# Attention scores with the lo parts of the queries on half the array's rows, two matmuls side by side, and the attention stage in a fixed order

## The chip, the cores and the metric

One core of a Trainium2 chip runs the whole kernel: one launch, float32 in and out. The core has five engines that run beside each other, each taking its own list of instructions in order: TensorE (PE, matmuls and transposes; PEld is its weight load), VectorE (DVE), ScalarE (ACT), GpSimd (POOL) and SyncE (SP), which issues transfers. Matmuls write to PSUM, eight banks of 128 x 512 float32; DVE and ACT read from there. The metric is the device time of one execution in microseconds, the median of several runs.

## What is computed

An encoder block over 2048 positions of width 1024: an input projection, differential attention with four heads beside Fourier mixing, an output projection, and a gated MLP. What concerns us here is the attention, cut to its core:

```python
def block(args):                       # one block of 128 queries
    qi, i = args                       # q, k: (B, S, 4 heads, 2 components, 64)
    dist = jnp.abs(pos_q[:, None] - pos_k[None, :])
    s = jnp.einsum('bqhcd,bkhcd->bhcqk', qi, k) * scale
    s = s - slopes[None, :, None, None, None] * dist[None, None, None]
    p = jax.nn.softmax(s, axis=-1)
    a = p[:, :, 0] - lam * p[:, :, 1]
    return jnp.einsum('bhqk,bkhv->bqhv', a, v)
```

Every head has two components c of queries and keys, each 64 wide. Each gives its own 128 x 2048 scores and softmax; the second, scaled by lam, is taken from the first, and the difference weighs the values.

## The kernel before, in words

To keep float32 accuracy with matmuls that round their operands, every operand is split in a hi part (rounded) and a lo part (what is left); products of hi with hi, hi with lo and lo with hi are summed. `split` (L77) makes the two: ACT copies hi out (L81), DVE subtracts to get lo (L82), so a lo always waits for its hi. `mm3` (L119) issues the three matmuls.

`in_proj` writes queries and keys to scratch in memory (`qd`, `kd`), transposed, each head and component as 64 rows of hi and 64 rows of lo. `load_k` brings a head's keys to SBUF so that partitions 0 to 63 hold hi and 64 to 127 lo. `load_q` puts the same 64 query rows on both halves of the partitions. One matmul of 128 rows with the hi part of the queries so gives hi x hi + hi x lo; one with the lo part gives lo x hi, and lo x lo beside it.

The attention stage runs over 64 units (4 heads times 16 blocks of 128 queries), in steps t, four to a unit; n = t // 4 is the unit whose scores are made. For a unit n:

- `scores` (L543): for each component c and each half of the keys (1024 wide), four matmuls (L567) into a PSUM tile s of two banks; there are two such tiles. DVE then adds slope times distance and keeps the running minimum mn (L572; `red0` for the first half, `red1` for the second, whose start value is red0's minimum). After the second half ACT takes the exponential over all 2048 columns with mn as bias and sums it (L576).
- `combine` (L579): DVE makes 1/sum (rr, L583) and the coefficient cf (L585); POOL and ACT scale the second component (L441, L443, L444) and POOL adds the two (L589).
- `transposes` (L591), two units later: four groups g of four 128 x 128 transposes into a PSUM tile pt (two tiles), each followed by a `split`: hi on ACT, lo on DVE. They give the transposed weights `at`.
- `values` (L602): `mm3` of `at` with the values of the head, two units (a pair) at a time, six matmuls 256 wide in each step.
- `finish` (L611): squares and scales a pair's output.

Tile positions, buffers and waits come from the framework. It also puts the instructions in each engine's order, by its own reckoning of when things are ready; `issue_after` (L130) ties one instruction behind another on the same engine where the author wants it. Before the change the attention stage has no such tie in its inner work, and the order is the framework's. While the first two units run, Fourier mixing still goes on (`fourier`, which advances the stage by `next(attention)`).

Of the kernel before, what the change touches and what calls it, by code (L numbers as in the profile page):

```python
# [11 lines left out]
F32 = mybir.dt.float32  # L12
# [3 lines left out]
AF = mybir.ActivationFunctionType  # L16
ALU = mybir.AluOpType
# [3 lines left out]
P = 128  # L21
D = 1024
S = 2048
NB = S // P
KB = D // P
H = 4
DH = 64
# [3 lines left out]
HALF = 512  # L31
# [4 lines left out]
SLOPES = [2.0 ** (-8.0 * (h + 1) / H) for h in range(H)]  # L36
# [4 lines left out]
class Block:  # L41
# [76 lines left out]

    def mm3(self, ps, terms, first=True, last=True, again=False):  # L119


        mm = functools.partial(self.nc.tensor.matmul, ps, skip_group_check=again)
        n = len(terms)
        for i, (ah, al, bh, bl) in enumerate(terms):
            mm(ah, bh, start=first and i == 0, stop=False)  # L125
            mm(ah, bl, start=False, stop=False)  # L126
            r = mm(al, bh, start=False, stop=last and i == n - 1)  # L127
        return r
# [9 lines left out]
    def in_proj(self, es_u, es_f):  # L138
# [3 lines left out]
        with ExitStack() as es, ExitStack() as es01:  # L142
# [47 lines left out]
            with ExitStack() as esn:  # L190
# [21 lines left out]
                r = {}  # L212
# [37 lines left out]
            for blk, b, gs in ((1, 0, range(4)), (1, 1, range(4)), (0, 0, (0, 1)), (0, 1, (0, 1)),  # L250
# [7 lines left out]
                for g in gs:  # L258
                    row = p.tile([P, HALF], F32, tag="row", name=f"row{blk}{b}{g}")
                    nc.sync.dma_start(row, self.rsd[g * HALF:(g + 1) * HALF].partition_broadcast(P))  # L260
                    for hh in range(2):
# [8 lines left out]
                            row, ALU.mult, ALU.mult)  # L270
                        self.split(z, st[:, 0, :], st[:, 1, :])
                        for c in range(2):
                            (nc.scalar if blk or gs[-1] < 3 else nc.sync).dma_start(
                                dst[h, c, :, :, g * HALF:(g + 1) * HALF].rearrange("l d t -> d l t").bitcast(F32),
                                st[c * DH:(c + 1) * DH].bitcast(F32))
# [179 lines left out]
    def load_k(self, h):  # L455
        t = self.slot(self.K_SLOT[h], [2, S], f"k{h}")
        for c in range(2):
            self.nc.gpsimd.dma_start(t[:, c], self.kd[h, c].rearrange("l d t -> (l d) t"))
        return t
# [71 lines left out]
    def attention(self, pss):  # L531

        nc, a = self.nc, self.a
        with ExitStack() as es:
# [7 lines left out]

            def scores(n, c, half):  # L543
                h, i = units[n]
                if c == 0 and half == 0:
                    if i % 4 == 2 and n + 2 < NU:
# [13 lines left out]
                if half == 0:  # L560
                    zs[n, c] = zp.tile([P, S], F32, tag=f"z{c}", name=f"z{n}_{c}")
                zt, qt, kt = zs[n, c], qs[h, i // 4], ks[h]
                ps = pss.tile([P, 1024], F32, tag="s", name=f"s{n}_{c}{half}")
                for l in range(2):
                    for j in range(2):
                        k0 = half * 1024 + j * HALF
                        nc.tensor.matmul(ps[:, j * HALF:(j + 1) * HALF], qt[:, 2 * c + l, i % 4 * P:i % 4 * P + P],  # L567
                                         kt[:, c, k0:k0 + HALF], start=l == 0, stop=l == 1)
                d0 = (NB - 1 - i) * P + half * 1024
                m0 = c * 2 + half  # L570

                nc.vector.tensor_tensor_reduce(  # L572
                    zt[:, half * 1024:(half + 1) * 1024], ps, dist[:, d0:d0 + 1024], SLOPES[h],
                    3.0e38 if half == 0 else mn[:, m0 - 1:m0], ALU.add, ALU.min, mn[:, m0:m0 + 1])
                if half == 1:
                    nc.scalar.activation(zt, zt, AF.Exp, bias=mn[:, 2 * c + 1:2 * c + 2], scale=-1.0,  # L576
                                         accum_out=ss[:, c:c + 1])

            def combine(n, half):  # L579
                z, z1, ss, rr = zs[n, 0], zs[n, 1], sums[n][1], recips[n // 2][:, n % 2, :]  # L580
                x = slice(half * 1024, (half + 1) * 1024)
                if half == 0:
                    nc.vector.reciprocal(rr, ss)  # L583
                    cfs[n] = sp.tile([P, 1], F32, tag="cf", name=f"cf{n}")
                    nc.vector.tensor_scalar(cfs[n], ss[:, 0:1], neglam[:, 0:1], rr[:, 1:2], ALU.mult, ALU.mult)  # L585
                    self.scale_half(0, z1[:, x], cfs[n])
                else:
                    self.scale_half(1, z1[:, x], cfs.pop(n))
                nc.gpsimd.tensor_tensor(z[:, x], z[:, x], z1[:, x], ALU.add)  # L589

            def transposes(n, g):  # L591
# [4 lines left out]
                for j in range(4):  # L596
                    kb = g * 4 + j
                    nc.tensor.transpose(pt[:, j * P:(j + 1) * P], zs[n, 0][:, kb * P:(kb + 1) * P], self.ident)  # L598
                us = slice(n % 2 * P, n % 2 * P + P)
                self.split(pt.rearrange("p (j t) -> p j t", j=4), at[:, :, 0, us], at[:, :, 1, us])  # L600

            def values(pr, kbs):  # L602
                h = units[2 * pr][0]
                if kbs[0] == 0:
# [3 lines left out]
                                           ats[pr, kb // 4][:, kb % 4, 1, :]) for kb in kbs],  # L608
                         first=kbs[0] == 0, last=kbs[-1] == NB - 1)

# [44 lines left out]

            LAG, outs, cfs = 2, {}, {}
            for t in range(4 * (NU + LAG + 4)):
                if t < 4 * LAG:
                    yield
                elif t == 4 * LAG:  # L660
# [489 lines left out]
```

## Time and profile before

| what | value |
|---|---|
| median of 3 runs | 2571.65 us (2568.43 to 2571.72) |
| the profiled execution's own time | 2574.7 us |
| its span, first to last instruction | 2572.9 us |
| PE busy | 2516.6 us, 98% |
| PEld busy | 2114.6 us, 82% |
| DVE busy | 1752.6 us, 68% |
| ACT busy | 1301.9 us, 51% |
| POOL busy | 716.9 us, 28% |
| first and last start of a score matmul | 410.3 and 954.8 us |
| first and last start of a transpose of attention | 427.4 and 972.4 us |
| mean granted clock of TensorE | 0.992 |

Lines of the profile's groups name the line of the kernel, the engine, the operation, the tile written and the tiles read, the shape and the count; then the busy time of the group, the mean duration of one in ns, and the idle time ahead of them with what ended it. Lines of a timeline give start and length in us, the same names, and in brackets the idle time just before, with what ended it. Matmuls overlap in the pipeline, so the sum of their lengths is more than the time they take; the step from one start to the next is the better measure. Rows of stretches give the busy time of PE, PEld, DVE, ACT and POOL, then the granted clock, the share of the transfer engines, and GB/s.

### The profile page before, as it was taken

How to read it: one execution, taken by the hardware profiler on the slowest of the kernel's cores; microseconds unless marked ns; L12 is line 12 of the kernel's file. 1: busy time of each engine (PE TensorE's matmuls, PEld its weight loads, DVE VectorE, ACT ScalarE, POOL GpSimd, SP SyncE). 2: the span in 40 equal slices, each digit the busy share in tenths (PEclk: the TensorE clock that was granted, in tenths of full speed). 3: DMA queues.
4: the chain of work that ended last, by engine and by line, in shares of the span. 5: the costliest groups of instructions: out<-in, count | busy, mean ns of one | idle time of the engine just before them, and what ended most of it. 6: DMA issues, size and time to landing. Idle time of an engine off the chain costs nothing.

```text
span 2572.9 us, 34950 instructions
## 1 busy us (share of the span) xinstructions
PE 2516.6 (98%) x13021; PEld 2114.6 (82%) x13021; DVE 1752.6 (68%) x2691; ACT 1301.9 (51%) x2036; POOL 716.9 (28%) x797
## 2 busy tenths in 40 slices
PE   9999999999999999978999999999999999999998
PEld 9998877888888888866888888877888888888886
DVE  4533358988889996786877777657777777434443
ACT  6321246888888883233544454444454445333332
POOL 1300015888988883271010010000000000000000
PEclk9999999999999999988999999999999999999999
DMA  8335558343332205554222221454212222546463
GB/s 264 98 125 139 152 143 237 66 74 73 74 75 50 48 26 173 181 174 140 107 74 79 88 79 70 160 181 155 91 74 76 88 83 85 185 137 219 146 204 113
DMA packets 146154, 309.12 MB, mean 120 GB/s; under 512 B 12080, under 2 KB 69440, under 8 KB 138816
## 3 DMA queue, kind: packets, MB, share of 16 engines
q1 hardware_dynamic: 90816, 226.60, 26.2%
q0 software_dynamic: 18256, 34.57, 6.7%
q10 hardware_dynamic: 36912, 45.72, 5.8%
q8 instruction: 102, 1.67, 0.3%
q14 instruction: 68, 0.56, 0.1%
HBM read 225.05 MB, written 81.80 MB: 119 GB/s over the span
## 4 chain that ended last, share of the span: by engine, by line
PE 87%; DVE 5%; DMA 4%; issue 1%; POOL 1%; ACT 1%; SPq 0%; POOLq 0%; ACTq 0%; DVEq 0%
PE s L567 9%; PE pd L127 5%; PE pd L125 5%; PE pd L126 5%; PE pt L598 4%; PE o L125 3%; PE o L127 3%; PE o L126 3%; PE pz L125 2%; PE pz L127 2%; PE pz L126 2%; DMA hb<-htd 2%; PE pv L127 1%; PE pv L126 1%; PE pv L125 1%
## 5 line engine op out<-in xcount | busy, mean ns | idle before, releaser
L589 POOL TENSOR_TENSOR z<-z,z 128x1024 f32<-128x1024 f32 x128 | 307.1, 2414 | 0.1
L82 DVE TENSOR_TENSOR d<-wd,d 128x512 fp32r<-128x512 f32 x240 | 157.0, 689 | 211.7 <-ACT d L81 211.4
L567 PE MATMUL s<-k,q 128*128 128x512 f32 x1024 | 281.5, 396 | 3.0 <-DVE mn L572 2.0
L576 ACT ACTIVATE z<-z,mn 128x2048 f32<-128x2048 f32 x128 | 257.5, 2012 | 33.7 <-DVE mn L572 32.7
L81 ACT ACTIVATE d<-wd 128x512 fp32r<-128x512 f32 x240 | 141.8, 626 | 236.9 <-PE pd L127 186.2
L125 PE MATMUL pd<-d,d 128*128 128x512 f32 x640 | 251.8, 393 | 1.9 <-ACT d L81 1.4
L127 PE MATMUL pd<-d,d 128*128 128x512 f32 x640 | 251.2, 393 | 0.5 <-DVE d L82 0.5
L126 PE MATMUL pd<-d,d 128*128 128x512 f32 x640 | 251.5, 393 | 0.0
L567 PEld LDWEIGHTS s<-k,q 128*128 128x128 f32 x1024 | 174.5, 188 | 29.4 <-DVE mn L572 5.0
L572 DVE CUSTOM_DVE_ANT_0 z<-s,dist,mn 128x1024 f32<-128x1024 f32 x128 | 163.8, 1280 | 38.6 <-PE s L567 37.8
L82 DVE TENSOR_TENSOR at<-pt,at 128x512 fp32r<-128x512 f32 x256 | 169.9, 686 | 8.5 <-ACT at L81 8.4
L81 ACT ACTIVATE at<-pt 128x512 fp32r<-128x512 f32 x256 | 147.5, 592 | 48.2 <-PE pt L598 44.8
L125 PE MATMUL o<-at,v 128*128 128x256 f32 x512 | 162.0, 316 | 0.0
L598 PE MATMUL pt<-ident,z 128*128 128x128 f32 x1024 | 156.7, 276 | 5.1 <-DVE at L82 5.1
L572 DVE CUSTOM_DVE_ANT_0 z<-s,dist 128x1024 f32<-128x1024 f32 x128 | 155.8, 1217 | 5.4 <-PE s L567 4.4
L598 PEld LDWEIGHTS pt<-ident,z 128*128 128x128 f32 x1024 | 125.7, 144 | 36.3 <-issue 10.5
L98 POOL TENSOR_SCALAR y_rs<-y_rs 128x1 f32<-128x1 f32 x16 | 6.9, 429 | 524.9 <-ACT sq L95 524.9
L126 PE MATMUL o<-at,v 128*128 128x256 f32 x512 | 146.3, 286 | 0.0
L125 PEld LDWEIGHTS pd<-d,d 128*128 128x128 f32 x640 | 120.1, 188 | 30.6 <-ACT d L81 1.8
L127 PEld LDWEIGHTS pd<-d,d 128*128 128x128 f32 x640 | 120.1, 188 | 29.0 <-DVE d L82 1.4
L127 PE MATMUL o<-at,v 128*128 128x256 f32 x512 | 143.7, 281 | 0.0
L126 PEld LDWEIGHTS pd<-d,d 128*128 128x128 f32 x640 | 120.1, 188 | 27.7 <-DVE d L82 0.3
(1058 smaller groups left out, 6895.0 us busy)
## 6 DMA issues: line engine op xcount, KB each, us to landing
wu<-in_w_up SPq DMA_DIRECT2D x44, 1024.0 KB, 4.8
wd<-in_w_down SPq DMA_DIRECT2D x88, 512.0 KB, 3.6
wd<-gd SPq DMA_DIRECT2D x88, 256.0 KB, 3.9
q<-qd POOLq DMA_DIRECT2D x32, 512.0 KB, 7.0
gd<-t SPq DMA_DIRECT2D x22, 512.5 KB, 2.6
gd<-t SPq DMA_DIRECT2D x22, 511.5 KB, 3.1
wst<-in_w_in SPq DMA_DIRECT2D x72, 128.0 KB, 3.6
xt<-in_xt SPq DMA_DIRECT2D x16, 512.0 KB, 4.6
```

Source lines behind the costliest of these rows:

```text
L81: r = nc.scalar.activation(hi, src, AF.Copy)
L82: return r, (lo_engine or nc.vector).tensor_tensor(lo, src, hi.bitcast(F32), ALU.subtract)
L98: nc.gpsimd.tensor_scalar(t[:, 1:2], t[:, 0:1], 1.0 / D, EPS, ALU.mult, ALU.add)
L125: mm(ah, bh, start=first and i == 0, stop=False)
L126: mm(ah, bl, start=False, stop=False)
L127: r = mm(al, bh, start=False, stop=last and i == n - 1)
L567: nc.tensor.matmul(ps[:, j * HALF:(j + 1) * HALF], qt[:, 2 * c + l, i % 4 * P:i % 4 * P + P], kt[:, c, k0:k0 + HALF], start=l == 0, stop=l ...
L572: nc.vector.tensor_tensor_reduce(zt[:, half * 1024:(half + 1) * 1024], ps, dist[:, d0:d0 + 1024], SLOPES[h], 3.0e38 if half == 0 else mn[: ...
L576: nc.scalar.activation(zt, zt, AF.Exp, bias=mn[:, 2 * c + 1:2 * c + 2], scale=-1.0, accum_out=ss[:, c:c + 1])
L589: nc.gpsimd.tensor_tensor(z[:, x], z[:, x], z1[:, x], ALU.add)
L598: nc.tensor.transpose(pt[:, j * P:(j + 1) * P], zs[n, 0][:, kb * P:(kb + 1) * P], self.ident)
```

## The change

Three things change, all for the attention stage.

The scratch of the keys is split in two halves of the sequence, and in the second half hi and lo change places. After loading, partitions 0 to 63 hold hi for the first 1024 keys and lo for the others; partitions 64 to 127 the reverse. The hi x (hi + lo) matmuls use all 128 rows as before. The lo part of the queries now meets only the hi part of the keys, on 64 rows: the upper rows for the first half of the keys, the lower rows for the second. The two halves' lo matmuls follow each other in turn, into different PSUM tiles; lo x lo is no longer computed. `load_k` issues four transfers for a head in place of two.

`scores` makes both halves of a component in one step (every second step), takes both PSUM tiles at once, and then has both reductions. The exponential becomes a function of its own, `exps`, called behind the transposes of the step. Both parts of `combine` are called in the first step of the next unit.

The new `behind` ties the matmuls, transposes and value matmuls on PE, the reductions, reciprocals and lo parts on DVE, and the exponentials and hi parts on ACT in the order in which the code is written.

```diff
-        self.kd = dt("kd", [H, 2, 2, DH, S])
+        self.kd = dt("kd", [H, 2, 2, 2, DH, S // 2])
...
-                        self.split(z, st[:, 0, :], st[:, 1, :])
+                        swap = blk and g // 2
+                        self.split(z, st[:, swap, :], st[:, 1 - swap, :])
...
         for c in range(2):
-            self.nc.gpsimd.dma_start(t[:, c], self.kd[h, c].rearrange("l d t -> (l d) t"))
+            for half in range(2):
+                self.nc.gpsimd.dma_start(t[:, c, half * 1024:(half + 1) * 1024],
+                                         self.kd[h, c, half].rearrange("l d t -> (l d) t"))
...
+            def behind(r, key):
+                if key in last:
+                    self.issue_after(r, last[key])
+                last[key] = r
+                return r
...
-                for l in range(2):
-                    for j in range(2):
-                        k0 = half * 1024 + j * HALF
-                        nc.tensor.matmul(ps[:, j * HALF:(j + 1) * HALF], qt[:, 2 * c + l, i % 4 * P:i % 4 * P + P],
-                                         kt[:, c, k0:k0 + HALF], start=l == 0, stop=l == 1)
...
+                for half in range(2):
+                    for j in range(2):
+                        behind(nc.tensor.matmul(out(half, j), qt[:, 2 * c, u], kt[:, c, cols(half, j)],
+                                                start=True, stop=False), "PE")
+                for j in range(2):
+                    for half in range(2):
+                        r = slice(half * DH, (half + 1) * DH)
+                        behind(nc.tensor.matmul(out(half, j), qt[r, 2 * c + 1, u], kt[r, c, cols(half, j)],
+                                                start=False, stop=True), "PE")
...
-                if half == 1:
-                    nc.scalar.activation(zt, zt, AF.Exp, bias=mn[:, 2 * c + 1:2 * c + 2], scale=-1.0,
-                                         accum_out=ss[:, c:c + 1])
...
+            def exps(n, c):
+                mn, ss = sums[n]
+                behind(nc.scalar.activation(zs[n, c], zs[n, c], AF.Exp, bias=mn[:, 2 * c + 1:2 * c + 2], scale=-1.0,
+                                            accum_out=ss[:, c:c + 1]), "ACT")
...
-                n, c, half = t // 4, t // 2 % 2, t % 2
-                if n < NU:
-                    scores(n, c, half)
+                n = t // 4
+                if n < NU and t % 2 == 0:
+                    scores(n, t // 2 % 2)
...
-                if n < NU and t % 4 == 3:
-                    combine(n, 0)
                 if 0 <= n - LAG < NU:
                     transposes(n - LAG, t % 4)
+                if n < NU and t % 2 == 0:
+                    exps(n, t // 2 % 2)
                 if 0 <= n - 1 < NU and t % 4 == 0:
+                    combine(n - 1, 0)
                     combine(n - 1, 1)
```

How the instructions then stand is shown at unit 32, in the middle of the stage. Names carry the unit and what it is: z32_0 the first component of unit 32, pt30_1 group 1 of the transposes of unit 30, s32_10 the scores of component 1, half 0.

ACT before, from the copy of group 0 to that of the next unit's group 0:

```order
L81 ACTIVATE at30_0_7423<-pt30_0_7424 128x4x128
L443 ACTIVATE z31_1_7353<-z31_1_7353,cf31_7387 128x512
L81 ACTIVATE at30_1_7447<-pt30_1_7448 128x4x128
L576 ACTIVATE z32_0_7407,ss32_7405<-z32_0_7407,mn32_7404 128x2048
L81 ACTIVATE at30_2_7468<-pt30_2_7469 128x4x128
L81 ACTIVATE at30_3_7494<-pt30_3_7495 128x4x128
L576 ACTIVATE z32_1_7461,ss32_7405<-z32_1_7461,mn32_7404 128x2048
L81 ACTIVATE at30_0_7423<-pt31_0_7517 128x4x128
```

And ACT in the change, over the same work:

```order
L82 ACTIVATE at30_0_7430<-pt30_0_7431 128x4x128
L599 ACTIVATE z32_0_7408,ss32_7406<-z32_0_7408,mn32_7405 128x2048
L447 ACTIVATE z31_1_7359<-z31_1_7359,cf31_7440 128x512
L82 ACTIVATE at30_1_7453<-pt30_1_7454 128x4x128
L82 ACTIVATE at30_2_7480<-pt30_2_7481 128x4x128
L599 ACTIVATE z32_1_7467,ss32_7406<-z32_1_7467,mn32_7405 128x2048
L82 ACTIVATE at30_3_7495<-pt30_3_7496 128x4x128
L82 ACTIVATE at30_0_7430<-pt31_0_7524 128x4x128
```

The scaling of the unit before and the copy of group 1 have moved from ahead of the first exponential to behind it, and the copy of group 3 from ahead of the second to behind it.

DVE in the change, from the lo part of group 0 to the first reduction of the next unit (ISA with z is a reduction, ISA with mn alone the read-out of its minimum):

```order
L83 TENSOR_TENSOR at30_0_7430<-pt30_0_7431,at30_0_7430 128x4x128
L606 RECIPROCAL rr30_7207<-ss31_7310 128x2
L608 TENSOR_SCALAR cf31_7440<-ss31_7310,neglam_70,rr30_7207 128x1
L83 TENSOR_TENSOR at30_1_7453<-pt30_1_7454,at30_1_7453 128x4x128
L593 ISA z32_1_7467,mn32_7405<-s32_10_7468,dist_4062 128x1024
L593 ISA mn32_7405 128x1
L593 ISA z32_1_7467,mn32_7405<-s32_11_7469,dist_4062,mn32_7405 128x1024
L593 ISA mn32_7405 128x1
L83 TENSOR_TENSOR at30_2_7480<-pt30_2_7481,at30_2_7480 128x4x128
L83 TENSOR_TENSOR at30_3_7495<-pt30_3_7496,at30_3_7495 128x4x128
L593 ISA z33_0_7511,mn33_7509<-s33_00_7512,dist_4062 128x1024
```

On DVE the lo part of group 1 stands ahead of the second component's reductions and that of group 3 ahead of the next unit's, as before; what has moved is that the first component's two reductions now follow each other directly, with the lo part of group 0, the reciprocal and the coefficient behind both.

PE in the change, a step with scores:

```order
L582 MATMUL s32_00_7409<-k2_6189,q2_0_7202 128x512 x2
L582 MATMUL s32_01_7410<-k2_6189,q2_0_7202 128x512 x2
L587 MATMUL s32_00_7409<-k2_6189,q2_0_7202 128x512
L587 MATMUL s32_01_7410<-k2_6189,q2_0_7202 128x512
L587 MATMUL s32_00_7409<-k2_6189,q2_0_7202 128x512
L587 MATMUL s32_01_7410<-k2_6189,q2_0_7202 128x512
L621 MATMUL pt30_0_7431<-ident_60,z30_0_7208 128x128 x4
L126 MATMUL o14_7385<-at28_1_7253,v1_5784 128x256
```

Before, four score matmuls stood in each step, all of 128 rows; now eight stand in every second one, the last four (L587) of 64 rows each and in turn for the two halves.

More of the change, by code (lines that the diff above doesn't have):

```diff
@@ L117, in transpose_split, with mm3 @@
         return last
-    def mm3(self, ps, terms, first=True, last=True, again=False):
+    def mm3(self, ps, terms, first=True, last=True, again=False, order=lambda r: r):
         mm = functools.partial(self.nc.tensor.matmul, ps, skip_group_check=again)
@@ L124, in mm3 @@
         for i, (ah, al, bh, bl) in enumerate(terms):
-            mm(ah, bh, start=first and i == 0, stop=False)
-            mm(ah, bl, start=False, stop=False)
-            r = mm(al, bh, start=False, stop=last and i == n - 1)
+            order(mm(ah, bh, start=first and i == 0, stop=False))
+            order(mm(ah, bl, start=False, stop=False))
+            r = order(mm(al, bh, start=False, stop=last and i == n - 1))
         return r
@@ L270, in in_proj @@
                             row, ALU.mult, ALU.mult)
-                        self.split(z, st[:, 0, :], st[:, 1, :])
+                        swap = blk and g // 2
+                        self.split(z, st[:, swap, :], st[:, 1 - swap, :])
                         for c in range(2):
+                            d = (dst[h, c, g // 2, :, :, g % 2 * HALF:(g % 2 + 1) * HALF] if blk
+                                 else dst[h, c, :, :, g * HALF:(g + 1) * HALF])
                             (nc.scalar if blk or gs[-1] < 3 else nc.sync).dma_start(
-                                dst[h, c, :, :, g * HALF:(g + 1) * HALF].rearrange("l d t -> d l t").bitcast(F32),
+                                d.rearrange("l d t -> d l t").bitcast(F32),
                                 st[c * DH:(c + 1) * DH].bitcast(F32))
@@ L541, in attention, with scores @@
             zs, sums, recips, ats, pos = {}, {}, {}, {}, {}
-            def scores(n, c, half):
+            def behind(r, key):
[3 more added lines that the diff above has]
+                return r
+            def scores(n, c):
                 h, i = units[n]
-                if c == 0 and half == 0:
+                if c == 0:
                     if i % 4 == 2 and n + 2 < NU:
@@ L569, in scores @@
[L569 to L574, printed above, removed]
-                if half == 1:
-                    nc.scalar.activation(zt, zt, AF.Exp, bias=mn[:, 2 * c + 1:2 * c + 2], scale=-1.0,
-                                         accum_out=ss[:, c:c + 1])
+                mn = sums[n][0]
@@ new lines, in scores @@
+                zt = zs[n, c] = zp.tile([P, S], F32, tag=f"z{c}", name=f"z{n}_{c}")
+                qt, kt = qs[h, i // 4], ks[h]
+                u = slice(i % 4 * P, i % 4 * P + P)
+                ps = [pss.tile([P, 1024], F32, tag="s", name=f"s{n}_{c}{half}") for half in range(2)]
+                cols = lambda half, j: slice(half * 1024 + j * HALF, half * 1024 + (j + 1) * HALF)
+                out = lambda half, j: ps[half][:, j * HALF:(j + 1) * HALF]
+                for half in range(2):
+                    for j in range(2):
+                        behind(nc.tensor.matmul(out(half, j), qt[:, 2 * c, u], kt[:, c, cols(half, j)],
+                                                start=True, stop=False), "PE")
@@ new lines, in scores @@
+                for j in range(2):
[3 more added lines that the diff above has]
+                                                start=False, stop=True), "PE")
+                d0 = (NB - 1 - i) * P
+                for half in range(2):
+                    m0 = c * 2 + half
+                    behind(nc.vector.tensor_tensor_reduce(
+                        zt[:, half * 1024:(half + 1) * 1024], ps[half], dist[:, d0 + half * 1024:d0 + (half + 1) * 1024],
+                        SLOPES[h], 3.0e38 if half == 0 else mn[:, m0 - 1:m0], ALU.add, ALU.min, mn[:, m0:m0 + 1]), "DVE")
@@ L582, in combine @@
                 if half == 0:
-                    nc.vector.reciprocal(rr, ss)
+                    behind(nc.vector.reciprocal(rr, ss), "DVE")
                     cfs[n] = sp.tile([P, 1], F32, tag="cf", name=f"cf{n}")
@@ L597, in transposes @@
                     kb = g * 4 + j
-                    nc.tensor.transpose(pt[:, j * P:(j + 1) * P], zs[n, 0][:, kb * P:(kb + 1) * P], self.ident)
+                    behind(nc.tensor.transpose(pt[:, j * P:(j + 1) * P], zs[n, 0][:, kb * P:(kb + 1) * P], self.ident), "PE")
                 us = slice(n % 2 * P, n % 2 * P + P)
-                self.split(pt.rearrange("p (j t) -> p j t", j=4), at[:, :, 0, us], at[:, :, 1, us])
+                hi, lo = self.split(pt.rearrange("p (j t) -> p j t", j=4), at[:, :, 0, us], at[:, :, 1, us])
+                behind(hi, "ACT")
+                behind(lo, "DVE")
             def values(pr, kbs):
@@ L608, in values @@
                                            ats[pr, kb // 4][:, kb % 4, 1, :]) for kb in kbs],
-                         first=kbs[0] == 0, last=kbs[-1] == NB - 1)
+                         first=kbs[0] == 0, last=kbs[-1] == NB - 1, order=lambda r: behind(r, "PE"))
             def finish(pr, stage):
@@ L654, in attention @@
             loading = {}
-            LAG, outs, cfs = 2, {}, {}
+            LAG, outs, cfs, last = 2, {}, {}, {}
             for t in range(4 * (NU + LAG + 4)):
```

4 lines of the change are left out of this document (removed).

## The prediction

> **What bounds the kernel now.** I read the page first: its span and its busy shares. Then the busy times of the stretch in which attention runs evenly, then the chain of waits in that stretch, and last the timelines of the engines, row by row, over one unit (128 queries of one head).
>
> ```profile
> span 2572.9 us, 34950 instructions
> core 0: us, PE busy (x) PEld busy (x) DVE busy (x) ACT busy (x) POOL busy (x), PEclk, DMA share, GB/s
> 500.00:920.00 420.00, 419.74 (x2848) 373.96 (x2847) 376.24 (x716) 356.49 (x496) 370.06 (x323) 1.00 0.31 61
> by line: PE s L567 43.0%; PE pt L598 21.1%; PE o L125 11.1%; PE o L127 10.9%; PE o L126 10.8%; PE o L624 2.0%; issue 0.7%; DVE z L572 0.4%; DVE at L82 0.2%; DVE mn L572 0.0%; DVE wo_x L82 0.0%
> ```
>
> TensorE is busy all through these 420 us, and the chain is its own instructions, one behind the other: scores, transposes, values. But the others are close: DVE has 376.24 us of work in 420. So what TensorE saves can only be had if the other three still keep up, and an order in which they wait for each other would be seen at once.
>
> The first DVE row of unit 2 and that of unit 63 give the pace:
>
> ```profile
> 428.89 1.21 DVE L572 CUSTOM_DVE_ANT_0 z<-s,dist 128x1024 f32<-128x1024 f32 x1
> ...
> 949.30 1.22 DVE L572 CUSTOM_DVE_ANT_0 z<-s,dist 128x1024 f32<-128x1024 f32 x1
> ```
>
> 520.41 us for 61 units: **8.53 us a unit**. Now one unit on DVE (start, length), and the same time on ACT, with one DVE row more at the end:
>
> ```profile
> 751.16 1.22 DVE L572 CUSTOM_DVE_ANT_0 z<-s,dist 128x1024 f32<-128x1024 f32 x1
> ...
> 752.69 0.69 DVE L82 TENSOR_TENSOR at<-pt,at 128x512 fp32r<-128x512 f32 x1
> 753.30 1.28 DVE L572 CUSTOM_DVE_ANT_0 z<-s,dist,mn 128x1024 f32<-128x1024 f32 x1
> 754.50 0.08 DVE L572 DVE_READ_ACCUMULATOR2_ANT mn<- 128x1 f32 x1
> 754.50 0.69 DVE L82 TENSOR_TENSOR at<-pt,at 128x512 fp32r<-128x512 f32 x1
> 755.38 1.23 DVE L572 CUSTOM_DVE_ANT_0 z<-s,dist 128x1024 f32<-128x1024 f32 x1 [0.18 <-PE s L567]
> 756.52 0.09 DVE L572 DVE_READ_ACCUMULATOR2_ANT mn<- 128x1 f32 x1
> 757.45 1.28 DVE L572 CUSTOM_DVE_ANT_0 z<-s,dist,mn 128x1024 f32<-128x1024 f32 x1 [0.84 <-PE s L567]
> ...
> 758.66 1.28 DVE L82 TENSOR_TENSOR at<-pt,at 128x512 fp32r<-128x512 f32 x2
> 759.86 1.22 DVE L572 CUSTOM_DVE_ANT_0 z<-s,dist 128x1024 f32<-128x1024 f32 x1
> ...
> 761.39 0.69 DVE L82 TENSOR_TENSOR at<-pt,at 128x512 fp32r<-128x512 f32 x1 [0.23 <-ACT at L81]
> ```
>
> ```profile
> 753.73 0.60 ACT L81 ACTIVATE at<-pt 128x512 fp32r<-128x512 f32 x1
> 754.68 2.01 ACT L576 ACTIVATE z<-z,mn 128x2048 f32<-128x2048 f32 x1 [0.35 <-DVE mn L572]
> ...
> 756.69 0.58 ACT L81 ACTIVATE at<-pt 128x512 fp32r<-128x512 f32 x1
> 757.88 0.60 ACT L81 ACTIVATE at<-pt 128x512 fp32r<-128x512 f32 x1 [0.62 <-PE pt L598]
> 758.78 2.01 ACT L576 ACTIVATE z<-z,mn 128x2048 f32<-128x2048 f32 x1 [0.29 <-DVE mn L572]
> ...
> 760.78 0.58 ACT L81 ACTIVATE at<-pt 128x512 fp32r<-128x512 f32 x1
> 762.11 0.60 ACT L81 ACTIVATE at<-pt 128x512 fp32r<-128x512 f32 x1 [0.75 <-PE pt L598]
> 762.60 0.71 ACT L443 ACTIVATE z<-z,cf 128x512 f32<-128x512 f32 x1
> 763.22 0.37 ACT L618 ACTIVATE osq<-o 128x256 f32<-128x256 f32 x1
> ```
>
> I call the two DVE reductions of one pass (one of the two score components c) red0 and red1, ACT's copy of transposed weights hi and DVE's remainder lo, numbered by group. See that the exponential starts as soon as red1 of its pass is read out, and that before it in ACT's queue stand copies that wait for TensorE alone. In this order hi0, hi1 come ahead of the first exponential, hi2, hi3 ahead of the second.
>
> And one step of TensorE:
>
> ```profile
> 754.24 1.10 PE L567 MATMUL s<-k,q 128*128 128x512 f32 x4
> 755.18 0.60 PE L598 MATMUL pt<-ident,z 128*128 128x128 f32 x4
> 755.53 0.37 PE L125 MATMUL o<-at,v 128*128 128x256 f32 x1
> ...
> 756.32 1.09 PE L567 MATMUL s<-k,q 128*128 128x512 f32 x4
> ```
>
> Four score matmuls take 0.94 us (0.235 each), four transposes 0.35, six value matmuls 0.79. The transposes of 755.18 are over by 755.78, yet their copy starts at 756.69, just behind the exponential: ACT takes its instructions strictly as they stand, and a long one ahead holds those behind it.
>
> **The change part by part.** *Matmuls.* Of eight score matmuls of a pass, four (lo part of the queries) now use 64 rows each, two by two. Side by side they save two times 0.235 us a pass, 0.94 us a unit, and leave TensorE 8.53 - 0.94 = 7.59 us of work; one after the other they save nothing. The trace has no such pair, so both ends stay.
>
> *Order.* This is the part that decides. In the change hi1 stands behind the first exponential and hi3 behind the second, while lo1 stands ahead of the second pass's reductions on DVE and lo3 ahead of the next unit's. Before, both stood ahead of those exponentials, and one ring went round once a unit (red1, exponential, hi2, hi3, lo3, next red0, next red1): 1.35 + 2.01 + 0.49 + 0.61 + 0.61 + 2.14 = 7.21 us with the steps below, 762.60 - 762.11 from copy to next and 753.30 - 751.16 from red0 to red1. That is under 8.53, so TensorE set the pace. Now there is a **ring through ACT and DVE, twice a unit**: red0, red1, exponential, hi, lo, and only then the next red0. Its terms, start to start:
>
> - red0 to red1: red0 is read out at 756.52 + 0.09, 1.23 after its start; red1 needs that value, and the nearest row of an instruction that needs a small result of its own engine starts 0.03 us after it (rr, cf below). I take 1.25. Ends: 1.14 if it could start with the read-out, 1.33 with the 0.10 us seen between 754.58 and the exponential.
> - red1 to exponential: 754.68 - 753.30 = 1.38, 758.78 - 757.45 = 1.33. I take 1.35.
> - exponential to the next on ACT: 756.69 - 754.68 = 2.01.
> - in the first pass only, the scaling of the unit before (L443) stands between: 763.22 - 762.60 = 0.62.
> - hi to lo: 761.39 - 760.78 = 0.61.
> - lo to the next reduction: 753.30 - 752.69 = 0.61, and half of 759.86 - 758.66, 0.60.
>
> First pass 1.25 + 1.35 + 2.01 + 0.62 + 0.61 + 0.61 = 6.45; second, without the scaling, 5.83 with 0.61. Sum **12.28 us a unit**, whatever TensorE does in it, since 7.59 or 8.53 both fit. Bounds by the two uncertain terms: 12.28 - 2 x 0.13 = 12.02 and 12.28 + 2 x 0.11 = 12.50.
>
> Does TensorE or POOL lengthen the ring? With red0 at 0, red1 ends at 2.53 and frees the second score buffer; the second pass's scores are done near 3.5 (4.0 one after the other) and needed at 6.45. The next unit's wait for the second pass's red1, over at 6.45 + 2.53 = 8.98, are done near 10.0 and needed at 12.28. POOL has 370.06 / 420 x 8.53 = 7.52 us a unit, starting from cf near 3.5: done near 11, needed by transposes that ACT copies only in the next unit. So none of them stands in the ring, and the whole saving on TensorE lies beside it.
>
> *Keys.* Loading a head's keys takes four transfers in place of two:
>
> ```profile
> L458 POOL DMA_DIRECT2D k<-kd x2 | 1.2, 597 | 0.0
> ```
>
> Two more issues of 0.6 us a head, on a POOL queue that now has some 4 us free a unit: nothing; 1.2 us a head if that were not so. The stores of the keys move as much as before, to other places.
>
> *Ends of the stage.* Before, the last coefficient is ready here:
>
> ```profile
> 958.73 0.17 DVE L583 RECIPROCAL rr<-ss 128x2 f32<-128x2 f32 x1 [0.90 <-ACT z L576]
> 958.93 0.27 DVE L585 TENSOR_SCALAR cf<-ss,neglam,rr 128x1 f32<-128x1 f32 x1
> ```
>
> That is 9.6 us after 949.30. In the change it stands behind the lo of the next step, at 12.28 + 0.6 + 0.2 = 13.1: 3.5 us later, with TensorE's last transposes behind it as before. In two units DVE has an output-weight split between the two reductions of a pass:
>
> ```profile
> 927.96 2.02 DVE L82 TENSOR_TENSOR wo<-wost,wo 128x512 fp32r<-128x512 f32 x1
> ```
>
> Between 0.7 and 2.0 us each in the ring: 2 us.
>
> **Sum.** 61 x (12.28 - 8.53) = 228.8; + 3.5 + 2 = 234 us. Against the profiled execution's own 2574.7 us: 2809. The median of the runs shown, 2571.65, lies 3 us under that execution, so 2806 us, **9% slower**. Bounds of the ring: 61 x 12.02 and 61 x 12.50 put it between 2790 and 2819; 5 us either way for the ends of the stage.
>
> **The rivals.**
>
> *The clock falls.* TensorE now waits in pieces. The longest: group 3 of the transposes needs the buffer that lo1 frees at 5.84 + 0.69 = 6.53 us, while the values ahead are done near 3.5 + 0.35 + 0.79 = 4.65, a gap of 1.9 us (1.4 if the pairs run one after the other). What gaps did in this trace:
>
> ```profile
> 1098.51 1.06 PE L754 MATMUL ht<-ident,hn 128*128 128x128 f32 x8 [1.83 <-ACT ms L81]
> 1770.41 0.50 PE L125 MATMUL pu_0a<-b,a_0p 128*128 128x512 f32 x1 [2.46 <-ACT xg L897]
> 1772.04 0.63 PE L125 MATMUL pu_0a<-b,a_0p 128*128 128x512 f32 x1
> 1771.00:1775.00 4.00, 4.00 (x12) 3.12 (x11) 1.89 (x2) 0.16 (x1) 0.10 (x1) 0.59 0.88 351
> 1100.00:1104.00 4.00, 4.00 (x19) 3.23 (x18) 3.79 (x6) 0.89 (x2) 4.00 (x4) 1.00 0.71 238
> 1800.00:2000.00 200.00, 200.00 (x863) 161.71 (x862) 153.66 (x199) 98.17 (x144) 16.47 (x40) 1.00 0.22 82
> ```
>
> After 1.83 us idle the granted clock stayed at 1.00; after 2.46 it fell to 0.59 over the next 4 us. A gap of 1.9 lies between. At half clock throughout, TensorE would need 2 x 7.59 = 15.2 us a unit, and the stage 61 x (15.2 - 8.53) = 407 us more: 2982. That can't hold, since TensorE without gaps gets its clock back (the 1800 row); with a fall in every second unit the scores are late by some 0.5 us a unit, 2836. I take that as this rival's time. The Trainium skill, TensorE: Matmul & The Clock Gate, Part 1, puts the drop at an idle window of about 3.4 us and asks for no gaps over some 3; by that there is no fall and the forecast stands, but the row of 2.46 us shows one sooner.
>
> *The saving is had.* If the ring did not close, because the copies came ahead of the exponential in time, the stage would go at the pace of the largest load: DVE, 376.24 / 420 x 8.53 = 7.64 us a unit, TensorE's 7.59 just under it. 61 x 0.89 = 54 us off: 2517. It decides from the point where a pass of the ring is under 3.8 us; the five terms make 5.8. For it speaks only that DVE and ACT are both under 90% busy now. The Trainium skill, same page, Part 3, says that matmuls on different row groups run at the same time; that is what TensorE's 7.59 would rest on, and no run here shows it yet. By it alone the kernel gains these 54 us; by the rows it gains nothing, since the ring doesn't pass through TensorE.
>
> *The pairs run one after the other.* TensorE then keeps 8.53 us, still under 12.28. The time is that of the forecast: the clock alone cannot tell, the starts of the paired matmuls can.
>
> **How the numbers follow.** Forecast (pairs side by side or not) 86%; the clock rival 8%; the saving had 3%, nothing changed 1%, and 2% for a longer ring that I haven't seen. The range takes in the ring's bounds and the clock rival: 2784 to 2840. About 0.2% is what a measurement of this kernel can tell from no change: faster 3%, same 1%, slower 96%.
>
> **What would show it.** Right: first reductions of successive units 12.0 to 12.5 us apart. On the ring's clock DVE has done lo0 and cf near 3.5 us and lo2 near 9.6, and starts lo1 at 5.84 and lo3 at 11.67: it idles 2.3 + 2.1 us a unit ahead of lo, waiting for ACT, some 270 us in all. ACT has done hi2 near 6.2 and hi0 of the next unit near 12.2, and the exponentials start at 9.05 and 14.88: about 5 us a unit, 300 us in all, waiting for DVE's mn. Further: TensorE near 62% busy in the stage; the gap ahead of transposes under 2 us and the clock at 1.00. The lo matmuls of a pair starting at nearly one time would show them side by side. Wrong: a unit under 9 us, or hi1 copied ahead of the exponential.

## The result, and the profile after

| | before | after |
|---|---|---|
| median of the runs side by side | 2570.48 us (2568.43 to 2571.72) | 2823.82 us (2820.76 to 2826.40) |
| span of the profiled execution | 2572.9 us | 2821.9 us |
| unit 2 to unit 63 of the stage | 520.41 us, 8.53 a unit | 765.71 us, 12.55 a unit |

The change makes the kernel slower by 9.8%: the ratio of its time to that before is 1.0981, 95% interval 1.0967 to 1.0995. The prediction of 2806 us was 18 us too low; the side and the mechanism were right.

From the page of the changed kernel, the span and the costliest groups of the stage (busy time, mean ns, then idle time ahead of them and whom it waited for):

```profile
span 2821.9 us, 35051 instructions
L599 ACT ACTIVATE z<-z,mn 128x2048 f32<-128x2048 f32 x128 | 256.8, 2006 | 289.1 <-DVE mn L593 289.1
L83 DVE TENSOR_TENSOR at<-pt,at 128x512 fp32r<-128x512 f32 x256 | 176.1, 688 | 269.8 <-ACT at L82 269.8
L621 PE MATMUL pt<-ident,z 128*128 128x128 f32 x1024 | 169.6, 289 | 128.6 <-DVE at L83 128.6
L582 PE MATMUL s<-k,q 128*128 128x512 f32 x512 | 179.9, 433 | 74.2 <-DVE mn L593 72.1
```

ACT waits for DVE, DVE waits for ACT, and TensorE waits for DVE: nobody is the bound, they pass one token round. The busy times of 500 us of the stage, and of the stretch from unit 2 to unit 63 (length, PE, PEld, DVE, ACT, POOL, then the clock), say the same:

```profile
500.00:1000.00 500.00, 371.41 (x2313) 262.41 (x2312) 311.62 (x579) 284.66 (x400) 302.75 (x270) 1.00 0.23 44
436.25:1201.96 765.71, 567.38 (x3506) 399.14 (x3506) 482.15 (x889) 437.41 (x616) 461.55 (x406) 1.00 0.22 45
```

No engine is over 75% busy, and the clock stays at 1.00. The chain of waits in those 500 us no longer holds TensorE at all:

```profile
by line: DVE z L593 39.3%; ACT z L599 29.6%; issue 11.6%; ACT at L82 7.8%; DVE at L83 5.8%; ACT z L447 4.9%; DVE mn L593 0.6%; DVEq L593 0.3%; ACTq L599 0.1%
```

One unit on DVE, from the first reduction of one to that of the next:

```profile
799.34 1.22 DVE L593 CUSTOM_DVE_ANT_0 z<-s,dist 128x1024 f32<-128x1024 f32 x1
800.48 0.08 DVE L593 DVE_READ_ACCUMULATOR2_ANT mn<- 128x1 f32 x1
800.71 1.28 DVE L593 CUSTOM_DVE_ANT_0 z<-s,dist,mn 128x1024 f32<-128x1024 f32 x1
...
805.32 0.69 DVE L83 TENSOR_TENSOR at<-pt,at 128x512 fp32r<-128x512 f32 x1 [2.33 <-ACT at L82]
805.92 1.21 DVE L593 CUSTOM_DVE_ANT_0 z<-s,dist 128x1024 f32<-128x1024 f32 x1
...
807.29 1.28 DVE L593 CUSTOM_DVE_ANT_0 z<-s,dist,mn 128x1024 f32<-128x1024 f32 x1
...
811.23 0.69 DVE L83 TENSOR_TENSOR at<-pt,at 128x512 fp32r<-128x512 f32 x1 [2.05 <-ACT at L82]
811.84 1.21 DVE L593 CUSTOM_DVE_ANT_0 z<-s,dist 128x1024 f32<-128x1024 f32 x1
```

and the same time on ACT:

```profile
802.09 2.00 ACT L599 ACTIVATE z<-z,mn 128x2048 f32<-128x2048 f32 x1 [0.47 <-DVE mn L593]
...
804.10 0.71 ACT L447 ACTIVATE z<-z,cf 128x512 f32<-128x512 f32 x1
804.71 1.06 ACT L82 ACTIVATE at<-pt 128x512 fp32r<-128x512 f32 x2
808.62 2.00 ACT L599 ACTIVATE z<-z,mn 128x2048 f32<-128x2048 f32 x1 [2.85 <-DVE mn L593]
...
810.62 1.06 ACT L82 ACTIVATE at<-pt 128x512 fp32r<-128x512 f32 x2
```

Follow the starts across the two fences: 799.34, 800.71 (DVE), 802.09, 804.10, 804.71 (ACT), 805.32, 805.92 (DVE): 1.37 + 1.38 + 2.01 + 0.61 + 0.61 + 0.60 = 6.58 us. The second pass: 805.92, 807.29, 808.62, 810.62, 811.23, 811.84: 1.37 + 1.33 + 2.00 + 0.61 + 0.61 = 5.92. Together 12.50, which is also the median of all units. TensorE meanwhile:

```profile
806.15 0.63 PE L621 MATMUL pt<-ident,z 128*128 128x128 f32 x4 [1.33 <-DVE at L83]
...
808.64 0.73 PE L582 MATMUL s<-k,q 128*128 128x512 f32 x2 [0.69 <-DVE mn L593]
809.30 0.74 PE L587 MATMUL s<-k,q 64*128 64x512 f32 x4
809.97 0.66 PE L621 MATMUL pt<-ident,z 128*128 128x128 f32 x4
```

Its scores are done at 810 and are first read at 811.84. The four lo matmuls do run two by two: in the trace's single records the first pair starts 3 ns apart, at 809.303 and 809.306, and the second pair in the same nanosecond, 809.644; over the stage 255 of the 256 pairs start within 8 ns. Yet the four take 0.67 us from the first start to the transposes behind them, not 2 x 0.235 = 0.47.

### The profile page after: what moved, and what is told of

Its sections match the earlier page's. It is cut to its first block, busy times and chain, and to the rows that moved or that the text cites. A ratio compares the mean times of both kernels' runs of the same rounds, so it can differ in the third digit from the quotient of the medians.

```text
span 2821.9 us, 35051 instructions
## 1 busy us (share of the span) xinstructions
PE 2565.4 (91%) x13021; PEld 2049.9 (73%) x13021; DVE 1767.8 (63%) x2691; ACT 1296.8 (46%) x2036; POOL 719.4 (25%) x805
## 4 chain that ended last, share of the span: by engine, by line
PE 61%; DVE 16%; ACT 12%; DMA 5%; issue 4%; POOL 1%; DVEq 0%; SPq 0%; ACTq 0%; POOLq 0%
DVE z L593 11%; ACT z L599 8%; PE pd L128 4%; PE pd L126 4%; PE pd L127 4%; ACT at L82 2%; PE pz L128 2%; PE pz L126 2%; PE pz L127 2%; DVE at L83 2%; DMA hb<-htd 1%; ACT z L447 1%; PE pv L127 1%; PE pv L128 1%; PE pv L126 1%
## 5 line engine op out<-in xcount | busy, mean ns | idle before, releaser
L599 ACT ACTIVATE z<-z,mn 128x2048 f32<-128x2048 f32 x128 | 256.8, 2006 | 289.1 <-DVE mn L593 289.1
L83 DVE TENSOR_TENSOR at<-pt,at 128x512 fp32r<-128x512 f32 x256 | 176.1, 688 | 269.8 <-ACT at L82 269.8
L621 PE MATMUL pt<-ident,z 128*128 128x128 f32 x1024 | 169.6, 289 | 128.6 <-DVE at L83 128.6
L621 PEld LDWEIGHTS pt<-ident,z 128*128 128x128 f32 x1024 | 109.6, 142 | 199.3 <-DVE at L83 103.2
L582 PE MATMUL s<-k,q 128*128 128x512 f32 x512 | 179.9, 433 | 74.2 <-DVE mn L593 72.1
L582 PEld LDWEIGHTS s<-k,q 128*128 128x128 f32 x512 | 78.0, 191 | 118.4 <-DVE mn L593 109.1
L82 ACT ACTIVATE at<-pt 128x512 fp32r<-128x512 f32 x256 | 136.5, 580 | 7.6 <-PE pt L621 7.5
```

The costliest lines, as they stand in the source:

```text
L82: r = nc.scalar.activation(hi, src, AF.Copy)
L83: return r, (lo_engine or nc.vector).tensor_tensor(lo, src, hi.bitcast(F32), ALU.subtract)
L582: behind(nc.tensor.matmul(out(half, j), qt[:, 2 * c, u], kt[:, c, cols(half, j)], start=True, stop=False), "PE")
L599: behind(nc.scalar.activation(zs[n, c], zs[n, c], AF.Exp, bias=mn[:, 2 * c + 1:2 * c + 2], scale=-1.0, accum_out=ss[:, c:c + 1]), "ACT")
L621: behind(nc.tensor.transpose(pt[:, j * P:(j + 1) * P], zs[n, 0][:, kb * P:(kb + 1) * P], self.ident), "PE")
```

## The experiments

Two theories stood against each other: that the **order** written out for ACT and DVE makes the whole loss, and that the **pairs** on TensorE make or take a part of it. All ratios are against the kernel before, run beside each kernel.

**1. The exponentials one step later.** They then stand behind the copy that the next lo needs.

```diff
-                if n < NU and t % 2 == 0:
+                if n < NU and t % 2 == 1:
                     exps(n, t // 2 % 2)
```

> The changed kernel with one edit: the exponential is called behind the transposes of the second step of its pass, so that hi1 stands ahead of the first exponential and hi3 ahead of the second, as before the change; pairs, ties and key layout stay. Ring theory: the ring through ACT and DVE closes once a unit instead of twice, no longer sets the pace, and a unit takes what TensorE needs, 8.2 to 8.6 us: 2555 to 2585 us. Rival (the half-array matmuls or the ties themselves are slow): the time stays over 2750 us.

2587.1 us, ratio 1.0064 (1.0052 to 1.0077); the median unit is 8.64 us. One line moved brings back 237 of the 253 us: the ring was the loss. It ended 2 us above the range, and what the pairs were to save has not appeared.

**2. The same without pairs**: every lo matmul on all 128 rows, so that lo x lo is computed again, as in the kernel before.

```diff
-   matmul(out(half, j), qt[r, 2 * c + 1, u], kt[r, c, cols(half, j)], ...)
+   matmul(out(half, j), qt[:, 2 * c + 1, u], kt[:, c, cols(half, j)], ...)
```

> As e1_exp_late, and the lo part of the queries meets all 128 rows of the keys again (it computes lo x lo as well), so no pairs. Ring theory: TensorE sets the pace at 8.5 us a unit, 2575 to 2595 us; the difference to e1_exp_late is what the pairs are worth where TensorE is the bound: 15 to 25 us, since in the changed kernel's trace a pass's 4 lo matmuls take 0.66 us and not 0.47, with 0.09 more ahead of them. If pairing gave its full 0.94 us a unit, e1 would be 58 us ahead of this one.

2590.92 us, ratio 1.0071 (1.0058 to 1.0084), a median unit of 8.71. The medians are 4 us apart, not the 15 to 25 expected, and the two intervals overlap: in this order the pairs hardly matter.

**3. The change without any ties**: the function `behind` only returns its instruction, and the framework sets the order.

> The changed kernel without its ties: the framework orders the instructions again; pairs and key layout stay, and the code order too. In the built order the copies hi1 and hi3 stand ahead of the exponentials in most units. Ring theory: under 8.8 us a unit, 2550 to 2600 us. Rival (pairs are slow): over 2750 us.

2609.86 us, ratio 1.0151 (1.0137 to 1.0165), 9.10 us a unit: the ring is gone, but 10 us over the range. Busy times of 400 us of its stage:

```profile
500.00:900.00 400.00, 399.65 (x2562) 298.85 (x2561) 345.00 (x646) 324.40 (x446) 335.49 (x296) 1.00 0.29 61
```

TensorE is busy throughout, and yet does less. In the order built here many lo matmuls stand one by one behind the hi matmuls of their own half: 212 of the 512 start with no partner within 10 ns. How much of the time over the range that makes was not tried by itself.

**4. The ring without pairs**: the change, with the edit of run 2.

> The changed kernel with its order, but the lo part of the queries on all 128 rows (lo x lo is computed as well): no pairs. Ring theory: TensorE isn't in the ring, the unit stays at 12.50 us and the time at 2824 us, within 8. Rival (the half-array matmuls are what costs): back near 2571 us.

2824.1 us in one run; median unit 12.50, mean 12.55. With the ring closed the pairs are worth nothing, as the forecast had it.

**5. One term less in the ring**: the scaling of L447 goes from ACT to POOL.

```diff
-   self.nc.scalar.activation(z[:, :HALF], z[:, :HALF], AF.Copy, scale=cf[:, 0:1])
+   self.nc.gpsimd.tensor_scalar(z[:, :HALF], z[:, :HALF], cf[:, 0:1], 0.0, ALU.mult, ALU.add)
```

> The changed kernel with the scaling of the second component's third quarter moved from ACT to POOL (same arithmetic). Ring theory: in the changed kernel's trace that instruction stands in the ring, 0.61 us from its start to the copy behind it; without it a unit takes 12.50 - 0.61 = 11.89 us, 62 units 38 us less: 2786 us, within 6. POOL has 7.5 us of work a unit and takes 0.7 more. Rival (the time is set by something else, TensorE's waits or the clock): no change, 2824 us.

2793.74 us, ratio 1.0873 (1.0836 to 1.0910), 2 us above the range; the mean unit is 11.99 and the median 11.89, as these two first reductions stand on DVE:

```profile
707.78 1.21 DVE L593 CUSTOM_DVE_ANT_0 z<-s,dist 128x1024 f32<-128x1024 f32 x1
...
719.67 1.21 DVE L593 CUSTOM_DVE_ANT_0 z<-s,dist 128x1024 f32<-128x1024 f32 x1
```

12.50 - 0.61 = 11.89: the unit gets shorter by just the term taken away, though in the changed kernel ACT waits 2.85 us for DVE ahead of the second exponential shown above. That is the mark of a ring.

**6. The ties alone**: the kernel before, its instructions tied in the order of its own code; four full score matmuls a step, the old keys.

> The kernel before, with ties in the order in which its own code is written, on the same instructions as the change ties; no pairs, old key layout, halves scored in their own steps. In its built order hi1 stands behind the first exponential and hi3 behind the second, and the reciprocal behind the second pass's red1. Ring theory: a ring closes twice a unit here too: 1.14 + 0.61 + 1.36 + 2.01 + 0.61 + 0.61 = 6.34 and 1.14 + 0.61 + 1.36 + 2.20 + 0.45 + 0.61 = 6.37, together 12.7 us a unit, 2571 + 61 x 4.2 = 2826 us, within 25. Rival (pairs and key layout are the cause): 2571 us.

2835.08 us, ratio 1.1033 (1.1001 to 1.1066), median unit 12.62. Neither pairs nor keys are needed for the loss; a fixed order in which exponentials precede copies is enough. This run also had what the clock rival spoke of, a regular gap ahead of the transposes and a lower clock over the stage:

```profile
644.23 0.66 PE L604 MATMUL pt<-ident,z 128*128 128x128 f32 x4 [1.93 <-DVE at L82]
```

```profile
500.00:700.00 200.00, 155.32 (x904) 131.50 (x903) 120.12 (x224) 110.41 (x154) 117.07 (x105) 0.91 0.24 47
```

The clock of 0.91 does not set the pace: the median unit still is the sum of the two passes of the ring, 6.34 + 6.28, as the first reductions of three passes in a row show:

```profile
701.74 1.21 DVE L578 CUSTOM_DVE_ANT_0 z<-s,dist 128x1024 f32<-128x1024 f32 x1
...
708.08 1.22 DVE L578 CUSTOM_DVE_ANT_0 z<-s,dist 128x1024 f32<-128x1024 f32 x1
...
714.36 1.21 DVE L578 CUSTOM_DVE_ANT_0 z<-s,dist 128x1024 f32<-128x1024 f32 x1
```

**7. The coefficient earlier.** Run 1 left 16 us over the kernel before. One idea: POOL gets its coefficient too late, since the reciprocal stands behind both reductions. Here reciprocal and coefficient of the unit before stand between red0 and red1.

```diff
+                    if c == 0 and half == 0 and n > 0:
+                        coefficient(n - 1)
...
```

> e1_exp_late with one more edit: the reciprocal and the coefficient of the unit before stand on DVE between the first pass's two reductions (where red1 waits 0.23 us for red0's minimum anyway), not behind lo0 and lo1. In e1's trace TensorE waits some 0.5 us a unit for POOL's sums, because the coefficient is ready only at the end of the pass. Theory (late coefficient is what keeps e1 behind the kernel before): a unit goes from 8.69 to 8.2 to 8.4 us, 2558 to 2575 us. Rival (e1 is bound by the score tiles' way through DVE): no change, 2587 us.

2583.38 us, ratio 1.0045 (1.0032 to 1.0057), a median unit of 8.63: the idea was wrong in the main. What holds it, on DVE and TensorE:

```profile
704.00 1.23 DVE L593 CUSTOM_DVE_ANT_0 z<-s,dist 128x1024 f32<-128x1024 f32 x1 [0.39 <-PE s L587]
...
705.54 1.28 DVE L593 CUSTOM_DVE_ANT_0 z<-s,dist,mn 128x1024 f32<-128x1024 f32 x1
...
706.88 0.30 PEld L582 LDWEIGHTS s<-k,q 128*128 128x128 f32 x2 [0.54 <-DVE mn L593]
...
707.54 0.73 PE L587 MATMUL s<-k,q 64*128 64x512 f32 x4
...
708.31 1.23 DVE L593 CUSTOM_DVE_ANT_0 z<-s,dist 128x1024 f32<-128x1024 f32 x1 [0.29 <-PE s L587]
```

The pair joins the two halves of a pass: both score tiles are finished by the last four matmuls. So red0 can't start before the second tile has been filled, and that tile is free only after red1 of the pass before. Red0, red1, second half's hi, pairs, red0: 4.31 us a pass here, 8.6 a unit, a ring again, with TensorE in it.

**8 and 9. Transposes between the hi matmuls of the two halves** (with and without pairs), to fill TensorE's wait for the second tile; the keys in two transfers.

```diff
                 for half in range(2):
...
+                    if half == 0:
+                        between()
...
-                    transposes(n - LAG, t % 4)
+                    copies(*(moved or transposes(n - LAG, t % 4)))
```

> e7_coef_early with two more edits: the transposes of a scoring step stand between the hi matmuls of the first and of the second half, so that the second score tile may come free later; and a head's keys come in two transfers again. Theory (in e1's trace TensorE's score matmuls wait for DVE's second minimum): TensorE works without waits, 8.0 to 8.3 us a unit, 2545 to 2565 us, faster than the kernel before. Rival (DVE's own work, 7.7 to 7.9 us with its waits for the scores, sets the pace): the same as e7_coef_early.

> e8_transposes_between with the lo part of the queries on all 128 rows of the keys (lo x lo is computed as well): no pairs. If TensorE sets the pace in e8, this one takes 8.5 us a unit and is 10 to 25 us slower than e8, and that is what the pairs are worth. If not, both take the same time.

2712.94 us, ratio 1.0547 (1.0533 to 1.0561), and 2717.13 us, ratio 1.0557 (1.0542 to 1.0573). This was badly wrong, by the same mistake as the change: a new order closed a longer ring. From the timeline of run 8:

```profile
700.57 1.28 DVE L83 TENSOR_TENSOR at<-pt,at 128x512 fp32r<-128x512 f32 x2
...
701.41 0.63 PE L629 MATMUL pt<-ident,z 128*128 128x128 f32 x4 [0.94 <-DVE at L83]
...
703.31 1.23 DVE L594 CUSTOM_DVE_ANT_0 z<-s,dist 128x1024 f32<-128x1024 f32 x1 [1.45 <-PE s L588]
...
706.05 1.28 DVE L83 TENSOR_TENSOR at<-pt,at 128x512 fp32r<-128x512 f32 x2
```

The transposes wait for a buffer that a lo behind the reductions must free, the pairs stand behind the transposes, and the next reduction waits for the pairs: 706.05 - 700.57 = 5.48 us here, 10.73 a unit in the median.

**10. Pairs within one half.** If what hurts is that a pair joins two tiles, its partners should lie in one tile. The keys are swapped by blocks of 512 columns, go in two transfers in the layout of before, and each half is finished by itself (the lines are shortened; every matmul is tied on PE as in the change):

```diff
-  for half in range(2):
-      for j in range(2):
-          matmul(out(half, j), qt[:, 2 * c, u], kt[:, c, cols(half, j)], start=True, stop=False)
-  for j in range(2):
-      for half in range(2):
-          r = slice(half * DH, (half + 1) * DH)
-          matmul(out(half, j), qt[r, 2 * c + 1, u], kt[r, c, cols(half, j)], start=False, stop=True)
+  for half, lo in ((0, 0), (0, 1), (1, 1), (1, 0)):
+      for j in range(2):
+          r = slice(j * DH, (j + 1) * DH) if lo else slice(0, P)
+          matmul(out(half, j), qt[r, 2 * c + lo, u], kt[r, c, cols(half, j)], start=half == lo, stop=half != lo)
```

> e7_coef_early with other pairs: the lo matmuls of the two 512-wide blocks of one half run side by side (hi and lo change places in every second block of 512 keys, so the keys load as before the change), and a pass goes: hi and pair of the first half, pair and hi of the second. Theory (in e7's trace red0 waits until both halves are done and the second half's matmuls wait for red1, a ring of 4.3 us a pass through the two score tiles): the first half is done 0.9 us ahead of the second, the ring opens, TensorE sets the pace with 4.03 us a pass and the small matmuls of finish, 8.2 to 8.3 us a unit: 2550 to 2565 us, faster than the kernel before by 5 to 20 us. Rival (something else holds e7): 2575 to 2590 us.

2563.67 us, ratio **0.9972** (0.9962 to 0.9982): the one kernel here that is clearly ahead of the kernel before, by 0.3%, with 8.42 us a unit on average (8.2 to 8.3 expected). TensorE is the bound again. Of the 20 us that separate it from run 7, 14 lie between unit 2 and unit 63 (513.8 us in place of 528.1); the others go with what comes ahead of unit 2, where the keys are back to two transfers. The gain is small, and the next run says why.

**11. The same without pairs.**

> e10_pairs_in_half with the lo part of the queries on all 128 rows of the keys (lo x lo is computed as well): same order, no pairs. If TensorE sets the pace in both, 8.5 to 8.6 us a unit, 2570 to 2585 us, and the pairs are worth 0.2 to 0.4 us a unit, 12 to 25 us, of the 0.94 that four matmuls fewer would be.

2568.55 us, ratio 0.9990 (0.9981 to 0.9998), 8.53 us a unit on average. So the pairs are worth some 5 us, not the 12 to 25 expected, and far from 61 x 0.94 = 57 us. Where the rest went stands in the rows of weight loads of one pass, in run 10 and in run 11:

```profile
702.78 0.31 PEld L580 LDWEIGHTS s<-k,q 128*128 128x128 f32 x2
703.45 0.30 PEld L580 LDWEIGHTS s<-k,q 64*128 64x128 f32 x4 [0.37 <-issue]
704.12 0.30 PEld L580 LDWEIGHTS s<-k,q 128*128 128x128 f32 x2 [0.37 <-issue]
704.46 0.59 PEld L621 LDWEIGHTS pt<-ident,z 128*128 128x128 f32 x4
```

```profile
702.48 1.70 PEld L580 LDWEIGHTS s<-k,q 128*128 128x128 f32 x8
704.22 0.59 PEld L621 LDWEIGHTS pt<-ident,z 128*128 128x128 f32 x4
```

Without pairs the weights of each matmul are loaded while the one ahead runs. At each change between 128 and 64 rows the load waits 0.37 us, though nothing in the profile holds it, and the matmul starts with its load. TensorE does not lose the 0.37 whole, since the matmul ahead still runs: from one start to the next it is 0.23 us between full matmuls, but 0.32 to 0.34 at each change and 0.34 at the step right behind it, some 0.2 us for a change in all (medians of 78 passes). From the first load to that of the transposes it is 1.68 us with pairs and 1.74 without: of the 0.47 us that a pass should save, 0.41 goes into the two changes of shape. Busy times do not show it: in 400 us of the stage TensorE is busy for 398 in both kernels.

## Why the prediction was right, and where its sizes were off

- **The ring.** Predicted 12.28 us a unit, through ACT and DVE twice; measured 12.50. Runs 1, 4, 5 and 6 show it from four sides: opened, it goes; without pairs it stays; shortened by 0.61 it follows by 0.61; made in the kernel before, it appears.
- **red0 to red1** is the term that was mis-sized: 1.25 taken, 1.33 as the upper end, 1.37 measured. The read-out ends at 800.48 + 0.08 = 800.56 and red1 starts at 800.71, 0.15 later; the rows of other small results (0.03) were the wrong neighbour. Twice 0.12, less 0.02 in the other terms, is 0.22 a unit, 13 us over 61 units. Every other term was right to 0.03.
- **Output-weight splits.** 2 us predicted. The units longer than 12.50 make 765.71 - 61 x 12.50 = 3.2: two with a split between the reductions, 1.15 and 1.11 over, and three others with 0.3 to 0.4 each, in which one red1 starts later; why is open.
- **Keys: nothing** was wrong at the first head. POOL issues the four transfers ahead of the distances, on which unit 0 waits. After, and then before:

```profile
393.07 2.37 POOL L463 DMA_DIRECT2D k<-kd  x4
...
396.66 0.59 POOL L535 DMA_DIRECT2D dist<-in_dist  x1
...
416.58 1.22 DVE L593 CUSTOM_DVE_ANT_0 z<-s,dist 128x1024 f32<-128x1024 f32 x1 [4.61 <-DMA dist<-in_dist]
```

```profile
392.03 1.33 POOL L458 DMA_DIRECT2D k<-kd  x2
...
394.88 0.57 POOL L529 DMA_DIRECT2D dist<-in_dist  x1
...
411.93 1.23 DVE L572 CUSTOM_DVE_ANT_0 z<-s,dist 128x1024 f32<-128x1024 f32 x1 [1.03 <-DMA dist<-in_dist]
```

  The first reduction is 4.7 us late. POOL came to the keys 1.0 us later; in the kernels here it does so at 391.8 to 395.0, whatever their transfers. From the first issue of keys to the first reduction it is 23.5 us in place of 19.9: 23.3 to 24.8 in the kernels with four transfers, 19.9 to 22.0 in those with two. So four transfers go with some 3.6 us. Units 0 and 1 add 2.7. They have no transposes of attention yet, so the ring is not closed in them; up to unit 2 DVE waits four times for a pass's scores, 3.5 us in all, which it did not do before. Unit 2 so starts 7.4 us late.
- **End of the stage.** Predicted 3.5 us later. The last transposes of attention start 27.6 us after unit 63's first reduction (1229.5 and 1201.96), in place of 23.1 (972.4 and 949.30): 4.5 later. The last coefficient starts 14.4 us after that reduction; 13.1 was predicted without the further output-weight splits that stand ahead of it on DVE.
- **Behind the stage: no term.** From the last transposes to the end of the span it took 1592 us in place of 1600, 8.2 less, though the change touches nothing there. The eleven other kernels take 1593.6 to 1597.4, whether the ring is closed in them or not. Why these two executions lie at the ends of the spread is open.
- **The sum.** 228.8 + 13.4 (ring) + 3.2 + 7.4 (start) + 4.5 (end) - 8.2 (behind) = 249 us, which is the difference of the two spans, against 234 predicted; the other 3 us are the step from the profiled execution to the median, which the changed kernel did not have. That start, end and what lies behind make 3.7 together, next to the 3.5 predicted for the end alone, is luck.
- **The views named as tests.** DVE ahead of lo: 270 us predicted, 269.8 on the page. ACT ahead of the exponentials: 300 and 289.1. TensorE 62% and 74%: with the 8.4 us a unit found below in place of 7.59 it would be 67%, and the page also counts the modelled end of the last matmul before each gap, which the sum of steps leaves out.
- **The clock.** The gap ahead of group 3's transposes was to be 1.9 us and is 1.33, since the values ahead of it end 5.48 us after red0 (806.15 - 1.33 - 799.34) and not 4.65; the clock kept 1.00. The Trainium skill, TensorE: Matmul & The Clock Gate, Part 1, puts the fall at idle times of some 3.4 us; run 6, whose longest gap in the window was 1.93 and whose clock stood at 0.91, goes against that. Its clock records show half clock in stretches of 3.41 us. From 500 to 900 us TensorE was busy for 43 to 51% of the 3.41 us ahead of each; in the changed kernel no such stretch holds less than 53%. So the share of work in a stretch fits better than the length of one gap, though in run 6 a few stretches as low as 46% were not followed by half clock.
- **The saving had.** Out of reach in the ring, as said, but not there outside it either: run 10 against 11. The figure of 7.59 us of TensorE work a unit, with which the prediction worked, is wrong: in run 10, where TensorE is the bound, a unit takes 8.42. It did not hurt the forecast, since neither is in the ring. The Trainium skill, TensorE: Matmul & The Clock Gate, Part 3, has matmuls on different row groups start together, and the trace agrees (within 8 ns). The Trainium skill, TensorEngine Tiling (Array Packing), Key Properties, says that a change of tiling mode drains the engine, without a figure. That agrees with the 0.37 us for which the load waits at each change; that a drain is what it waits for was not tried by itself.

## What to carry to other kernels

Before an order is fixed by hand, write down for each engine what stands behind its longest instruction, and follow who waits for that across the engines: if the walk comes back to its start within one unit, the sum of its starts is the pace, whatever the engines' busy times say. An operation that finishes two buffers at once makes one buffer of them, so a pair should end within one tile. And a change of matmul shape within a step is priced, by the rows of weight loads and the steps from one matmul to the next, before the matmuls it saves are counted.

## What the runs showed of the hardware

- Two matmuls of 64 rows on different halves of the array start within 8 ns of each other, but at the change from 128 to 64 rows and back the first weight load waits 0.37 us, and each change costs TensorE some 0.2 us (steps of 0.32 to 0.34 us in place of 0.23, run 10 against run 11).
- A reduction that needs the minimum of the one ahead on the same engine starts 0.15 us after the read-out's end (800.71 and 800.56).
- In run 6 TensorE waited 31 times for a lo in 200 us, 1.44 us on average and 1.93 at the longest, and the granted clock was 0.91. In the changed kernel it waited 80 times in 500 us, 0.99 on average and 1.6 at the longest, and the clock was 1.00. Ahead of each stretch of half clock in run 6 (3.41 us long) TensorE was busy for 43 to 51% of 3.41 us, and for no less than 53% anywhere in the changed kernel, from 500 to 900 us in both. That this share sets the clock was not tried by itself.
